# Value products of an attention stage in groups of four, three and three key tiles instead of two at a time

## The chip, the cores and the metric

The kernel runs on one core of one Trainium2 chip. The metric is the device time of the core in microseconds (us): the median over several executions. The kernel before takes 1477.8 us (median of 3 runs, 1475.59 to 1479.57).

## The reference

Two layers of a network over 1024 latent tokens behind a prefix of 256 context tokens, width 1024. Layer 0 mixes with gated recurrences and Fourier transforms; the change does not touch it. Layer 1 is attention with 16 heads, whose queries and keys have a part of 64 and a rotary part of 32, and whose output is gated and projected:

```python
def attend(q, k, v):
    s = jnp.einsum('bqhd,bkhd->bhqk', q, k, preferred_element_type=jnp.float32) * ATTN_SCALE
    p = jax.nn.softmax(s, axis=-1).astype(v.dtype)
    return jnp.einsum('bhqk,bkhd->bqhd', p, v)
...
    o_l = blocked_attention(q_l, k_all, v_all).reshape(b_, s_, MLA_WIDTH)
    y_lat = (o_l * jax.nn.silu(g_l)) @ w_out
```

The 1024 latent queries look at all 1280 keys; behind the attention come a residual and a layer normalisation.

## The kernel before

The attention stage works on 8 pairs of heads one after another (loop over `p`, L1116 on). A pair has two halves of 512 queries (`hf`), and a half has 10 key tiles of 128 keys (`kt`). The slot number `g` is 10 hf + kt, 0 to 19 within a pair. In the stage the order of work on TensorE, VectorE, ScalarE and GpSimd is the order in which the program issues it; each engine takes its own part in that order. The DMAs on the sync engine's queue (SP) are ordered by the framework.

At each key tile `attend` issues ten score matmuls into `s` (L1051): five products, each for the two heads of the pair in the upper and lower 64 rows of the array. ScalarE turns them into probabilities `p` (L1053, six buffers), and GpSimd adds these up into the row sums `ra` (L1057; in pair 7 GpSimd and VectorE share that, L1061, `ra` and `rv`). `pv` (L1067) issues the value products of one key tile: two matmuls, one for each head, each in its own 64 columns of the array, added up in `po`. A value matmul leaves two records in the trace. `finish` returns the rest of a half's work, which is issued in the next half at the key tiles named in its table: `rest` (the last value products and the product with the gate `sgt`, L1077), `rows` (the product of the row sums with ones, `rp`, L1084, copied to `ri` by ScalarE, L1087), four `piece` (a reciprocal of 128 columns each, L1092) and `last` (the product of `ri` and `sgt`, L1096, and the store to `o_dr`).

Between them stands work for the next pair, in the lists `near` (issued behind the scores) and `far` (issued last in a slot). The first slots have the key and query products (`pk`, `pq`), others the products of the next four heads (`pra`, `pv`, and on VectorE the scaling of `wk`, L882). From slot 2 on come the 24 units of `max_pass`: a unit multiplies 128 queries with 512 keys (or 256, every third) for the two heads (`mx`, L976) and VectorE reduces each head's tile to its maximum (`m`, L978). Behind the 24th, in slot 18, `mt` (L985) transposes the maxima `nm`. All these products take their tiles from one pool in turn:

```python
    m_ps, m_psc = pool("m_ps", 3, space=PSUM)
```

So a tile waits until the third tile before it has been read. `at_` is the table of the units' slots; an entry is the slot and 0 for `near`, 1 for `far`. One key tile is issued like this, with the value products of two key tiles at 3, 5, 7 and 9:

```python
                attend(p, hf, kt, st)
                for u in near[g]:
                    u()
                if kt > 2 and kt % 2:
                    pv(p, st, kt - 3)
                    pv(p, st, kt - 2)
                for u in tail.get(kt, ()):
                    u()
                for u in far[g]:
                    u()
```

Behind pair 7 stands the output projection `yf` (`out1`, L1191). Its first tile of tokens has the rest of the last half (`tail`) between its matmuls.

Of the kernel before, what the change touches and what calls it, by code (L numbers as in the profile page):

```python
# [27 lines left out]
NT = T // P  # L28
# [26 lines left out]
def _body(ctx, tc, ap, out, dbg=None):  # L55
# [947 lines left out]
    for m in range(8):  # L1003
# [3 lines left out]
        for q in range(2):  # L1007
            ps = s_ps.tile([P, 2, 512], F32, tag="s", name=f"in1g{m}{q}")[:, 0, :]
            c = slice(512 * q, 512 * q + 512)
# [54 lines left out]
    def pv(p, st, k):  # L1064
        q, i = divmod(p, 2)
        for a in range(2):
            TE.matmul(st["o"][64 * a : 64 * a + 64, :], quad[q][6][:, k, 128 * i + 64 * a : 128 * i + 64 * a + 64],  # L1067
                      st["e"][k][:, a, :], start=(k == 0), stop=(k == NT - 1), tile_position=(0, 64 * a))

    def finish(p, hf, st):  # L1070

        c = slice(512 * hf, 512 * hf + 512)

        def rest():
            for k in (8, 9):
                pv(p, st, k)
            V.tensor_tensor(out=st["sg"], in0=st["sg"], in1=st["o"], op=ALU.mult)  # L1077

        def rows():
            rp = m_ps.tile([P, 512], F32, tag="m", name=f"rp{p}{hf}")  # L1080
            sums = [st[n] for n in ("ra", "rv") if n in st]
            for j, r in enumerate(sums):
                for a in range(2):
                    TE.matmul(rp[64 * a : 64 * a + 64, :], ones, r[:, a, :], start=(j == 0), stop=(j == len(sums) - 1),  # L1084
                              tile_position=(0, 64 * a))
            st["ri"] = at.tile([P, 512], F32, tag="ri", name=f"ri{p}{hf}")
            S.copy(out=st["ri"], in_=rp)  # L1087

        def piece(b):
            def run():  # L1090
                d = slice(P * b, P * b + P)
                V.reciprocal(out=st["ri"][:, d], in_=st["ri"][:, d])  # L1092
            return run

        def last():
            V.tensor_tensor(out=st["sg"], in0=st["ri"], in1=st["sg"], op=ALU.mult)  # L1096
            load(o_dr[p][:, c], st["sg"])

        if p == 7 and hf == 0:
            return {1: [rest], 2: [rows], 3: [piece(0), piece(1)], 4: [piece(2)], 5: [piece(3), last]}  # L1100
        return {1: [rest], 3: [rows], 4: [piece(0)], 5: [piece(1)], 6: [piece(2)], 7: [piece(3)], 8: [last]}

    def o_load(t, p):
        orw = f1_p.tile([P, 8, P], F32, tag="raw", bufs=3, name=f"orw{t}")
# [4 lines left out]
        return oh, ol  # L1109

    vt[1] = at.tile([P, NT, 256], F32, name="v_odd")
    tail = {}
    for p in range(8):

# [2 lines left out]
        if p < 7:  # L1117
# [4 lines left out]
            near[1] += prep[3:4]  # L1122
            far[1] += prep[4:5]
            near[2] += prep[5:]
            at_ = [(g, b) for g in range(2, 2 * NT) for b in range(2) if not (g == 2 and b == 0) and (b == 0 or g % 2)]
            at_.insert(0, (2, 1))
            for (g, b), u in zip(at_, mx[:-1]):
                (far if b else near)[g].append(u)
            g = at_[len(mx) - 2][0]
# [34 lines left out]
        for hf in range(2):  # L1164
            st = {}
            for kt in range(NT):
                g = NT * hf + kt
                attend(p, hf, kt, st)
                for u in near[g]:
                    u()  # L1170
                if kt > 2 and kt % 2:
                    pv(p, st, kt - 3)
                    pv(p, st, kt - 2)
                for u in tail.get(kt, ()):
                    u()
                for u in far[g]:
                    u()
                if p == 7 and g == 18:
                    o0 = o_load(0, f1_p)
            tail = finish(p, hf, st)  # L1180
# [12 lines left out]

    H2 = [slice(0, 512), slice(512, D)]
    y0 = f_ps.tile([P, D], F32, tag="y", name="yf0")
    out1(*o0, [y0[:, c] for c in H2], H2, range(2), {1: tail[1], 3: tail[3]})
    for kt in sorted(tail)[2:]:
        for u in tail[kt]:
            u()
# [172 lines left out]
```

## Time and profile before

| What | Value |
|---|---|
| Median of 3 runs | 1477.8 us |
| The profiled execution | 1479.07 us |
| Its span, first to last instruction | 1477.3 us |
| Mean granted TensorE clock | 0.988 of full speed |
| Busy: TensorE, VectorE, ScalarE, GpSimd | 1409.1, 931.4, 539.9, 660.9 us |
| Attention stage, pairs 0 to 7 | about 842 to 1357 us |

All numbers are of one profiled execution. In a row of the timeline stand the start, the time from there to the end of the last of the merged instructions, the engine, the line, the operation with output and inputs, the shapes, how many instructions were merged, and in brackets how long the engine had been idle and what ended that. Matmuls overlap, so the distance of two starts tells what one costs. `DVE` is VectorE, `PE` TensorE, `ACT` ScalarE, `POOL` GpSimd.

### The profile page before, as it was taken

How to read it: one execution, taken by the hardware profiler on the slowest of the kernel's cores; microseconds unless marked ns; L12 is line 12 of the kernel's file. 1: busy time of each engine (PE TensorE's matmuls, PEld its weight loads, DVE VectorE, ACT ScalarE, POOL GpSimd, SP SyncE). 2: the span in 40 equal slices, each digit the busy share in tenths (PEclk: the TensorE clock that was granted, in tenths of full speed). 3: DMA queues.
4: the chain of work that ended last, by engine and by line, in shares of the span. 5: the costliest groups of instructions: out<-in, count | busy, mean ns of one | idle time of the engine just before them, and what ended most of it. 6: DMA issues, size and time to landing. Idle time of an engine off the chain costs nothing.

```text
span 1477.3 us, 19801 instructions
## 1 busy us (share of the span) xinstructions
PE 1409.1 (95%) x7912; PEld 1009.3 (68%) x7912; DVE 931.4 (63%) x1461; ACT 539.9 (37%) x664; POOL 660.9 (45%) x307
## 2 busy tenths in 40 slices
PE   6998999999999999998999999999999999998895
PEld 3776777787888788887976755655555555554674
DVE  5668878665765352239635365667566665767698
ACT  2276566666112221105421333443433434353110
POOL 1134334343211143303241187568767856675442
PEclk9999999999999999999999999999999999999998
DMA  8613233332303564210242211012101101033431
GB/s 307 232 51 110 97 111 111 111 103 76 123 29 126 188 192 140 92 52 22 89 137 71 72 33 51 15 37 59 39 22 38 57 16 37 15 95 113 159 131 74
DMA packets 65868, 134.09 MB, mean 91 GB/s; under 512 B 5864, under 2 KB 31720, under 8 KB 63472
## 3 DMA queue, kind: packets, MB, share of 16 engines
q1 hardware_dynamic: 63328, 124.83, 26.1%
q0 software_dynamic: 2016, 7.60, 1.4%
q8 instruction: 62, 1.02, 0.3%
q10 hardware_dynamic: 432, 0.39, 0.1%
q14 instruction: 30, 0.25, 0.1%
HBM read 101.14 MB, written 24.66 MB: 85 GB/s over the span
## 4 chain that ended last, share of the span: by engine, by line
PE 68%; DVE 20%; DMA 4%; issue 4%; ACT 2%; POOL 2%; SPq 0%; DVEq 0%; POOLq 0%; ACTq 0%
PE s L1051 11%; PE z L267 11%; PE y L646 10%; PE po L1067 9%; PE mx L976 6%; PE in1g L85 2%; PE in1g L87 2%; PE in1g L86 2%; DVE xc L317 2%; DVE hf L1246 1%; DVE th L362 1%; DVE gate L367 1%; DVE gate L378 1%; DVE hf L1236 1%; DMA woraw<-in_wo 1%
## 5 line engine op out<-in xcount | busy, mean ns | idle before, releaser
L1057 POOL TENSOR_TENSOR ra<-ra,p 128x1024 f32<-128x1024 f32 x112 | 269.2, 2403 | 96.3 <-ACT p L1053 93.1
L978 DVE TENSOR_REDUCE m<-mx 128x1 f32<-128x512 f32 (+1 forms) x384 | 210.1, 589 | 100.9 <-PE mx L976 100.5
L1053 ACT ACTIVATE p<-s 128x1024 f32<-128x1024 f32 x160 | 163.3, 1025 | 208.4 <-PE s L1051 208.3
L267 PE MATMUL z<-uh,w0h 128*128 128x512 f32 (+1 forms) x576 | 150.1, 368 | 4.3 <-ACT uh L76 4.3
L267 PE MATMUL z<-ul,w0h 128*128 128x512 f32 (+1 forms) x576 | 147.9, 362 | 0.0
L267 PE MATMUL z<-uh,w0l 128*128 128x512 f32 (+1 forms) x576 | 147.5, 361 | 0.0
L82 POOL TENSOR_TENSOR w0l<-w,w0h 128x1024 fp32r<-128x1024 f32 x24 | 63.9, 2664 | 185.4 <-DVE w0h L78 135.5
L267 PEld LDWEIGHTS z<-uh,w0h 128*128 128x128 f32 x576 | 98.7, 191 | 33.4 <-issue 10.7
L267 PEld LDWEIGHTS z<-ul,w0h 128*128 128x128 f32 x576 | 96.8, 190 | 18.6 <-issue 1.0
L267 PEld LDWEIGHTS z<-uh,w0l 128*128 128x128 f32 x576 | 96.4, 190 | 18.3 <-issue 2.0
L1051 PE MATMUL s<-R,KR 33*128 33x512 f32 (+1 forms) x640 | 101.5, 392 | 0.0
L345 ACT ACTIVATE gate<-gps,vec 128x512 f32<-128x512 f32 (+1 forms) x96 | 57.5, 616 | 104.3 <-PE gps L87 104.2
L976 PE MATMUL mx<-Kh,Qh 64*128 64x512 f32 (+1 forms) x384 | 83.4, 404 | 4.5 <-DVE m L978 4.5
L976 PEld LDWEIGHTS mx<-Kh,Qh 64*128 64x128 f32 x384 | 39.1, 185 | 69.4 <-DVE m L978 35.5
L1067 PE MATMUL po<-p,v_odd 128*64 128x512 f32 x320 | 77.5, 605 | 0.0
L1067 PE MATMUL po<-p,v_even 128*64 128x512 f32 x320 | 77.5, 605 | 0.0
L381 POOL TENSOR_TENSOR gate<-gate,gate 128x1280 f32<-128x1280 f32 x8 | 23.9, 2988 | 112.2 <-DVE gate L378 97.1
L976 PE MATMUL mx<-KR,R 64*128 64x512 f32 (+1 forms) x384 | 72.7, 356 | 0.0
L1051 PEld LDWEIGHTS s<-R,KR 33*128 33x128 f32 (+1 forms) x640 | 61.3, 184 | 13.1
L1051 PE MATMUL s<-Qh,Kh 64*128 64x512 f32 x320 | 69.9, 430 | 0.0
L649 DVE TENSOR_TENSOR n<-gbc,y 128x1024 f32<-128x1024 f32 x10 | 12.2, 1222 | 86.1 <-PE y L646 86.1
L1051 PE MATMUL s<-Ql,Kh 64*128 64x512 f32 x320 | 63.7, 391 | 0.0
(360 smaller groups left out, 3078.0 us busy)
## 6 DMA issues: line engine op xcount, KB each, us to landing
w<-in_w SPq DMA_DIRECT2D x24, 512.0 KB
adaw<-in_ada SPq DMA_DIRECT2D x32, 256.0 KB
adawm<-in_ada SPq DMA_DIRECT2D x8, 1024.0 KB
adawg<-in_ada_g SPq DMA_DIRECT2D x8, 1024.0 KB
y_dr<-sg SPq DMA_DIRECT2D x10, 640.0 KB
woraw<-in_wo SPq DMA_DIRECT2D x12, 512.0 KB
xt<-in_x_cm SPq DMA_DIRECT2D x8, 640.0 KB
yra<-y_dr SPq DMA_DIRECT2D x10, 512.0 KB
```

Of the source, the lines that this page charges most:

```text
L82: el.tensor_tensor(out=lo, in0=src, in1=f(hi), op=ALU.subtract)
L85: TE.matmul(o, lh, rh, start=start, stop=False)
L86: TE.matmul(o, lh, rl, start=False, stop=False)
L267: TE.matmul(z[:, a : a + n], wi[:, kt, :], ui[kt][:, a : a + n], start=(kt == 0 and ui is uh and wi is wh), stop=(kt == KT - 1 and wi is wl))
L345: S.activation(out=gt[d, g][:, a : a + n], in_=ps[:, :n], func=AF.Sigmoid, bias=vv("gateb", 4 * j + i))
L646: TE.matmul(ps[:, 512 * hf : 512 * hf + 512], a[k], b[k][:, 512 * hf : 512 * hf + 512], start=(k == 0 and a is yh and b is woh), stop=(k = ...
L976: TE.matmul(ps[a][:, :n], q[r, P * t : P * t + P], k[r, a0 : a0 + n], start=st, stop=not st)
L978: V.tensor_reduce(out=m3s[t][:, a, i : i + 1], in_=ps[a][:, :n], axis=AX.X, op=ALU.max)
L1051: TE.matmul(ps[:, a, :], k[r, ks], w[r, c], start=(j == 0), stop=(j == len(parts) - 1))
L1053: S.activation(out=es, in_=ps, func=AF.Exp, scale=SCALE)
L1057: G.tensor_tensor(out=ra, in0=st["e"][0] if kt == 1 else ra, in1=es, op=ALU.add)
L1067: TE.matmul(st["o"][64 * a : 64 * a + 64, :], quad[q][6][:, k, 128 * i + 64 * a : 128 * i + 64 * a + 64], st["e"][k][:, a, :], start=(k == ...
```

## The change

Value products are issued in three groups instead of five: those of key tiles 0 to 3 at key tile 5, those of 4 to 6 at key tile 8, and those of 7 to 9 in the next half at key tile 1. The product of the row sums moves from key tile 3 to 5, the four reciprocals from 4, 5, 6, 7 to 6, 7, 8, 9, and the last product from 8 to 9. In the table of the max units one `far` entry moves from slot 9 to slot 8. Between the two halves of pair 7 the table of `finish` stays as it is, but for the longer `rest`.

```diff
--- before.py
+++ after.py
@@ -1072,7 +1072,7 @@
         c = slice(512 * hf, 512 * hf + 512)
 
         def rest():
-            for k in (8, 9):
+            for k in PVL:
                 pv(p, st, k)
             V.tensor_tensor(out=st["sg"], in0=st["sg"], in1=st["o"], op=ALU.mult)
 
@@ -1098,7 +1098,7 @@
 
         if p == 7 and hf == 0:
             return {1: [rest], 2: [rows], 3: [piece(0), piece(1)], 4: [piece(2)], 5: [piece(3), last]}
-        return {1: [rest], 3: [rows], 4: [piece(0)], 5: [piece(1)], 6: [piece(2)], 7: [piece(3)], 8: [last]}
+        return {1: [rest], 5: [rows], 6: [piece(0)], 7: [piece(1)], 8: [piece(2)], 9: [piece(3), last]}
 
     def o_load(t, p):
         orw = f1_p.tile([P, 8, P], F32, tag="raw", bufs=3, name=f"orw{t}")
@@ -1109,6 +1109,9 @@
         return oh, ol
 
     vt[1] = at.tile([P, NT, 256], F32, name="v_odd")
+
+    PVG = {5: (0, 1, 2, 3), 8: (4, 5, 6)}
+    PVL = (7, 8, 9)
     tail = {}
     for p in range(8):
 
@@ -1122,8 +1125,7 @@
             near[1] += prep[3:4]
             far[1] += prep[4:5]
             near[2] += prep[5:]
-            at_ = [(g, b) for g in range(2, 2 * NT) for b in range(2) if not (g == 2 and b == 0) and (b == 0 or g % 2)]
-            at_.insert(0, (2, 1))
+            at_ = sorted([(g, 0) for g in range(3, 18)] + [(g, 1) for g in (2, 3, 5, 7, 8, 11, 13, 15, 17)])
             for (g, b), u in zip(at_, mx[:-1]):
                 (far if b else near)[g].append(u)
             g = at_[len(mx) - 2][0]
@@ -1168,9 +1170,8 @@
                 attend(p, hf, kt, st)
                 for u in near[g]:
                     u()
-                if kt > 2 and kt % 2:
-                    pv(p, st, kt - 3)
-                    pv(p, st, kt - 2)
+                for k in PVG.get(kt, ()):
+                    pv(p, st, k)
                 for u in tail.get(kt, ()):
                     u()
                 for u in far[g]:
@@ -1193,7 +1194,7 @@
 
     H2 = [slice(0, 512), slice(512, D)]
     y0 = f_ps.tile([P, D], F32, tag="y", name="yf0")
-    out1(*o0, [y0[:, c] for c in H2], H2, range(2), {1: tail[1], 3: tail[3]})
+    out1(*o0, [y0[:, c] for c in H2], H2, range(2), {1: tail[1], 3: tail[5]})
     for kt in sorted(tail)[2:]:
         for u in tail[kt]:
             u()
```

The places are shown in pair 1, second half. In the names `mx2710` is the max unit for pair 2, query tile 7, key piece 1, head 0; `s118` are the scores of pair 1, half 1, key tile 8; `p114` its probabilities of key tile 4. First TensorE at slot 17 (key tile 7), before:

```order
L976 MATMUL mx2710_7900<-Kh0_5775,Qh0_5773 128x512
L976 MATMUL mx2711_7901<-Kh0_5775,Qh0_5773 128x512
L976 MATMUL mx2710_7900<-KR1_5764,R10_5777 128x512
L976 MATMUL mx2711_7901<-KR1_5764,R10_5777 128x512
L1067 MATMUL po11_7663<-p114_7813,v_even_5769 64x512 x2
L1067 MATMUL po11_7663<-p115_7837,v_even_5769 64x512 x2
L976 MATMUL mx2720_7913<-Kh0_5775,Qh0_5773 128x256
L976 MATMUL mx2721_7914<-Kh0_5775,Qh0_5773 128x256
L976 MATMUL mx2720_7913<-KR1_5764,R10_5777 128x256
L976 MATMUL mx2721_7914<-KR1_5764,R10_5777 128x256
L1051 MATMUL s118_7922<-Qh1_6662,Kh1_6664 128x512 x2
```

and with the change:

```order
L976 MATMUL mx2710_7898<-Kh0_5775,Qh0_5773 128x512
L976 MATMUL mx2711_7899<-Kh0_5775,Qh0_5773 128x512
L976 MATMUL mx2710_7898<-KR1_5764,R10_5777 128x512
L976 MATMUL mx2711_7899<-KR1_5764,R10_5777 128x512
L976 MATMUL mx2720_7907<-Kh0_5775,Qh0_5773 128x256
L976 MATMUL mx2721_7908<-Kh0_5775,Qh0_5773 128x256
L976 MATMUL mx2720_7907<-KR1_5764,R10_5777 128x256
L976 MATMUL mx2721_7908<-KR1_5764,R10_5777 128x256
L1051 MATMUL s118_7916<-Qh1_6662,Kh1_6664 128x512 x2
```

The value group between the two units is gone: a unit of 512 keys is followed at once by one of 256, and that by the scores.

TensorE from slot 18 on, before:

```order
L985 MATMUL mt2_7936<-ident_60,nm2_7315 16x128
L1051 MATMUL s119_7944<-Qh1_6662,Kh1_6664 128x512 x2
L1051 MATMUL s119_7944<-Ql1_6663,Kh1_6664 128x512 x2
L1051 MATMUL s119_7944<-Qh1_6662,Kl1_6665 128x512 x2
L1051 MATMUL s119_7944<-R11_6666,KR1_5764 128x512 x2
L1051 MATMUL s119_7944<-R21_6667,KR2_5765 128x512 x2
L1067 MATMUL po11_7663<-p116_7873,v_even_5769 64x512 x2
L1067 MATMUL po11_7663<-p117_7897,v_even_5769 64x512 x2
```

and with the change:

```order
L985 MATMUL mt2_7930<-ident_60,nm2_7313 16x128
L1067 MATMUL po11_7661<-p114_7804,v_even_5769 64x512 x2
L1067 MATMUL po11_7661<-p115_7827,v_even_5769 64x512 x2
L1067 MATMUL po11_7661<-p116_7871,v_even_5769 64x512 x2
L1051 MATMUL s119_7943<-Qh1_6662,Kh1_6664 128x512 x2
```

The three value products of key tiles 4 to 6 now stand behind `mt`, and the group behind the scores of key tile 9 is gone.

VectorE over slots 16 to 18, before:

```order
L978 TENSOR_REDUCE m327_7876<-mx2700_7877 128x1
L978 TENSOR_REDUCE m327_7876<-mx2701_7878 128x1
L1092 RECIPROCAL ri10_7791<-ri10_7791 128x128
L978 TENSOR_REDUCE m327_7876<-mx2710_7900 128x1
L978 TENSOR_REDUCE m327_7876<-mx2711_7901 128x1
L1092 RECIPROCAL ri10_7791<-ri10_7791 128x128
L978 TENSOR_REDUCE m327_7876<-mx2720_7913 128x1
L978 TENSOR_REDUCE m327_7876<-mx2721_7914 128x1
L980 TENSOR_REDUCE nm2_7315<-m327_7876 128x2
L987 TENSOR_SCALAR mrow2_7938<-mt2_7936 16x128
L1096 TENSOR_TENSOR sgt10_7316<-ri10_7791,sgt10_7316 128x512
```

and with the change:

```order
L978 TENSOR_REDUCE m327_7874<-mx2700_7875 128x1
L978 TENSOR_REDUCE m327_7874<-mx2701_7876 128x1
L1092 RECIPROCAL ri10_7849<-ri10_7849 128x128
L978 TENSOR_REDUCE m327_7874<-mx2710_7898 128x1
L978 TENSOR_REDUCE m327_7874<-mx2711_7899 128x1
L1092 RECIPROCAL ri10_7849<-ri10_7849 128x128
L978 TENSOR_REDUCE m327_7874<-mx2720_7907 128x1
L978 TENSOR_REDUCE m327_7874<-mx2721_7908 128x1
L980 TENSOR_REDUCE nm2_7313<-m327_7874 128x2
L987 TENSOR_SCALAR mrow2_7932<-mt2_7930 16x128
L1092 RECIPROCAL ri10_7849<-ri10_7849 128x128 x2
L1096 TENSOR_TENSOR sgt10_7314<-ri10_7849,sgt10_7314 128x512
```

The reciprocals stand at the same two places among the reductions, but they are the first two pieces now (before, the last two), and two more follow ahead of the last product.

## Rows read from the trace of the kernel before

**Rows 1.** The page: busy time, share of span and instructions; the chain that ended last.

```profile
PE 1409.1 (95%) x7912; PEld 1009.3 (68%) x7912; DVE 931.4 (63%) x1461; ACT 539.9 (37%) x664; POOL 660.9 (45%) x307
...
PE 68%; DVE 20%; DMA 4%; issue 4%; ACT 2%; POOL 2%; SPq 0%; DVEq 0%; POOLq 0%; ACTq 0%
```

**Rows 2.** Windows view, pair 3: stretch, length, each engine's busy us, clock, DMA.

```profile
1040.40:1107.60 67.20, 67.20 (x438) 38.41 (x436) 41.73 (x74) 27.11 (x32) 45.53 (x20) 1.00 0.10 29
```

**Rows 3.** Timeline of TensorE, pair 6, slot 13 to the scores of slot 14.

```profile
1284.05 0.40 PE L1051 MATMUL s<-Qh,Kh 64*128 64x512 f32 x2
...
1285.21 0.40 PE L976 MATMUL mx<-Kh,Qh 64*128 64x512 f32 x2
1285.44 0.40 PE L976 MATMUL mx<-KR,R 64*128 64x512 f32 x2
1285.77 1.94 PE L1067 MATMUL po<-p,v_odd 128*64 128x512 f32 x8
1287.54 1.03 PE L1084 MATMUL rp<-ra,ones 128*64 128x512 f32 x4
1288.50 0.39 PE L976 MATMUL mx<-Kh,Qh 64*128 64x256 f32 x2
1288.72 0.28 PE L976 MATMUL mx<-KR,R 64*128 64x256 f32 x2
1288.84 0.39 PE L1051 MATMUL s<-Qh,Kh 64*128 64x512 f32 x2
```

**Rows 4.** Timeline of VectorE, the reductions of the unit at 1285.21.

```profile
1285.88 1.29 DVE L978 TENSOR_REDUCE m<-mx 128x1 f32<-128x512 f32 x2 [0.34 <-PE mx L976]
```

**Rows 5.** Timeline of TensorE, then VectorE, pair 2, slot 7.

```profile
998.65 0.39 PE L976 MATMUL mx<-Kh,Qh 64*128 64x512 f32 x1
1000.36 0.49 PE L976 MATMUL mx<-Kh,Qh 64*128 64x512 f32 x1 [1.32 <-DVE m L978]
...
1001.01 1.94 PE L1067 MATMUL po<-p,v_odd 128*64 128x512 f32 x8
...
996.98 2.72 DVE L882 TENSOR_SCALAR wk<-wk,vec 128x512 f32<-128x512 f32 x1
999.62 1.27 DVE L978 TENSOR_REDUCE m<-mx 128x1 f32<-128x512 f32 x2
```

**Rows 6.** Timeline of TensorE, pair 6, slot 9 to the scores of slot 10.

```profile
1275.59 0.38 PE L976 MATMUL mx<-Kh,Qh 64*128 64x256 f32 x1
1276.55 0.38 PE L976 MATMUL mx<-Kh,Qh 64*128 64x256 f32 x1 [0.58 <-DVE m L978]
...
1276.78 0.50 PE L1051 MATMUL s<-Qh,Kh 64*128 64x512 f32 x2
```

**Rows 7.** View of waits, 862 to 1350 us: total us, times, longest us.

```profile
PE mx L976 <- DVE m L978: 4.5, 4, 1.3
```

**Rows 8.** Timeline of VectorE, then TensorE, pair 6, slots 16 to 18.

```profile
1297.42 0.94 DVE L1092 RECIPROCAL ri<-ri 128x128 f32<-128x128 f32 x1
1298.28 1.22 DVE L978 TENSOR_REDUCE m<-mx 128x1 f32<-128x512 f32 x2
...
1300.28 0.69 DVE L978 TENSOR_REDUCE m<-mx 128x1 f32<-128x256 f32 x2
...
1301.21 0.28 PE L985 MATMUL mt<-ident,nm 128*16 128x128 f32 x1
```

**Rows 9.** View of line L1096: ns min, median, max; first and last start.

```profile
L1096 DVE TENSOR_TENSOR sgt<-ri,sgt x16: 669/1151/2781, 903.1 to 1371.0; 128x512 f32<-128x512 f32 x16
```

**Rows 10.** Timeline of VectorE, then TensorE, pair 3, slot 3.

```profile
1053.09 2.56 DVE L978 TENSOR_REDUCE m<-mx 128x1 f32<-128x512 f32 x4
...
1054.48 1.94 PE L1067 MATMUL po<-p,v_odd 128*64 128x512 f32 x8
```

**Rows 11.** Timeline of VectorE, then TensorE, pair 7 and its end.

```profile
1318.76 2.06 DVE L1061 TENSOR_TENSOR rv<-rv,p 128x1024 f32<-128x1024 f32 x1 [2.74 <-ACT p L1053]
...
1357.24 1.22 PE L1191 MATMUL yf<-w1oh,oh 128*128 128x512 f32 x2 [5.29 <-ACT oh L76]
```

## The prediction

> **What bounds the kernel now.** First the page: TensorE is busy 95% of the span, and the chain that ended last runs through it for 68% [rows 1]. Only the attention stage is touched, from about 842 us to 1375 us, so I read that stage pair by pair: in the 67.2 us of pair 3 TensorE is busy all the time, VectorE for 41.7 us, GpSimd for 45.5 us [rows 2]. An order of TensorE's work that has more gaps costs time one for one here, and one with fewer gains it; the other engines matter only where TensorE waits for them. The view of waits shows how little that is now: 4 waits of `mx` matmuls for VectorE, 4.5 us in all [rows 7]. Pair 7 is different: TensorE sits idle for 5.29 us before the output projection, and VectorE starts its `rv` work after 2.74 us of idleness and then stays busy [rows 11]; so VectorE, not TensorE, sets the end there.
>
> Durations below are of the profiled execution, 1479.07 us (its span of 1477.3 and 1.8 around it), 1.3 us over the median of the runs, 1477.8. I add the differences to the median.
>
> **The gain: fewer changes of tile shape.** Value products use two column tiles (128x64), scores and max products two row tiles (64x128). Entering a value group takes 0.33 us from the last `mx` start to the first `po` start, where the step within a shape is 0.23: 0.10 lost. Leaving costs twice: four records of `rp` take 0.96 where a record takes 1.77/8 = 0.22, so 0.08 lost, and the first 256-wide step afterwards is 0.22 instead of 0.12, 0.10 lost [rows 3]. Together 0.28 us a group. The order has 80 such groups before and 48 after: 28 fewer in pairs 0 to 6, on the path, 28 x 0.28 = 7.8 us, and 4 fewer in pair 7, which I cost at nothing, because VectorE sets the end there. The row sums' product stands directly behind a value group today already [rows 3], so that part saves nothing.
>
> **The loss: max units back to back.** Each pair runs 24 max units for the next one; eight slots hold two. Today a value group stands between the two at every one of them. Now the groups stand at key tiles 5 and 8 (and 1), and at key tiles 3 and 7 of both halves a 512-wide unit is followed at once by a 256-wide one. A unit takes two of the three buffers of `m_ps`, so the second unit's second tile needs the first unit's first buffer, and VectorE must have reduced that. The reduction starts 0.67 us after the unit's first matmul (1285.88 against 1285.21) and takes half of 1.29 us [rows 3, 4]; the waiting matmul starts 0.10 later (999.62 + 0.64 = 1000.26, against 1000.36) [rows 5]. So it starts at 0.67 + 0.64 + 0.10 = 1.41 us, and the scores follow 0.23 later (1276.55, 1276.78) [rows 6], at 1.64. Without a wait they would follow after two steps of 0.23 and two of 0.12, at 0.70. **Price: 0.94 us a place.** That TensorE really stops there is seen at 1000.36, where the same kind of tile waits while VectorE scales `wk` [rows 5]. At key tile 3 of the first half VectorE is already at work on four reductions: the third ends at 1053.09 + 3 x 0.64 = 1055.01, so the scores follow at 1055.34; with neither group nor wait they would at 1054.48 - 0.10 + 0.24 = 1054.62. There the price is 0.72 [rows 10]. With 4 places in each of 7 pairs that is 21 x 0.94 + 7 x 0.72 = 24.8 us. No row shows the pairing itself; the nearest are this 0.72 and the 1.8 us lost around 1000.36 (998.65 to 1001.01 is 2.36, where 0.46 + 0.10 would do). Between them I take the composed 0.94, since its three parts are measured.
>
> The Trainium skill has a rule against this change: TensorEngine Tiling (Array Packing), section PSUM Bottleneck, says that tiling speeds TensorE up but not the emptying of PSUM, which may then be the limit. The wait at 1000.36 agrees; by the rule the loss counts whole, and without it the sum would be the gain alone.
>
> **VectorE is later where the groups are gone.** The four reciprocal pieces (0.86 us from start to next start) move from key tiles 4 to 7 to key tiles 6 to 9, so that pieces fall where no value group covers them.
> - *Slots 16 to 18.* From the start of the unit at 16: its reductions run from 0.67 to 1.96, a piece to 2.82 [rows 4, 8]. The unit at 17 starts at 0.46 + 1.16 = 1.62 [rows 3], its first half is reduced at 3.46, and the scores follow at 3.79 instead of 2.32. VectorE ends the second half at 4.10, another piece at 4.96, the 256-wide pair (0.69) at 5.65, and `mt`, which stood 0.24 behind that pair, comes at 5.89; TensorE would be there at 3.79 + 1.16 + 0.10 = 5.05 [rows 3, 8]. Lost 1.47 + 0.84 = 2.31, of which 0.94 is counted: 1.37 x 7 = 9.6 us.
> - *Slots 6 to 8.* In odd pairs `pv` products after unit 6 give VectorE time for the first piece; after unit 7 the second runs to 2.82, the next reduction ends at 3.17, and unit 8 waits till 3.27 instead of 2.80: 0.47 x 3. Pair 6 has no such products: 0.50 + 0.47. Pairs 2 and 4 scale `wk` at this place, 2.72 us [rows 5], and lose the 1.8 there today; depending on whether the scaling takes half of that or all, the same walk gives -0.1 to +0.9 more, taken 0.4 each. Pair 0 has no pieces in its first half: -0.9. Sum 2.3 us.
> - *Slots 9 to 11.* The last product of a half (L1096) takes 0.67 to 2.78 us, median 1.15 [rows 9], and now comes right before units 10 and 11. At the short end nothing waits, at the long end 1.4 us is lost; I take 0.5 x 6, less the 0.85 that one of them costs today (1276.78 - 1275.59, less 0.34) [rows 6]: 2.1 us.
>
> L1096 has two inputs in SBUF. The Trainium skill, GPSIMD Engine Reference, Key points, says that GpSimd and VectorE instructions of that kind contend for SBUF; the spread in its row agrees, and by the rule the long end would hold wherever an addition to the row sums runs.
>
> **Pair 7.** The third key tile of the last group (4 x 0.22 = 0.9 us) moves behind the first projection matmuls and ahead of the last row sums, on which the end hangs: +0.9. Scores reach key tile 5 with 8 records and one group less before them, 2.0 us earlier; VectorE's 2.74 us of idleness can use it. I take 1.2, as ScalarE has weight casts between its exponentials, against 0.9 for the piece that moves behind: -0.3. Sum +0.6.
>
> **Costed at nothing.** The probabilities have six buffers: tile 0 is released at key tile 5, one ahead of the exponential that takes its buffer, and tiles 4 to 6 at key tile 8, two ahead. GpSimd's additions get two key tiles more before the row sums need them. On SP the store of a half moves one key tile later and the rotary copies queue behind it, by about 1 us; they are read first by the max unit in slot 2. If that cover fell short, 1 us a pair would be lost.
>
> **Sum:** -7.8 + 24.8 + 9.6 + 2.3 + 2.1 + 0.6 = **+31.6 us**; 1477.8 + 31.6 = 1509.
>
> **Rivals.**
> 1. *Only the gain counts* (the other side). The second unit finds its buffers free, because the reductions keep pace. 1477.8 - 7.8 + 0.6 = 1471. It decides at 7.8/28 = 0.28 us a place: below that the change wins. For it: VectorE is idle for a third of a pair [rows 2], and there are few waits today [rows 7]. Against: the 1.41 us to the release is arithmetic on three rows, and the wait at 1000.36 is of this very kind. Chance 0.10. The Trainium skill's TensorEngine Tiling (Array Packing), Key Properties, says that a change of tiling mode drains TensorE; that agrees with the 0.28, and taken alone it leads here.
> 2. *They cancel.* The places cost a third of what I say: 1478. Chance 0.06.
> 3. *Short waits.* 0.72 at every place, 20.2 us, the pieces fit into VectorE's idle time, and the 1.8 lost in pairs 0, 2 and 4 today goes into the new waits: -7.8 + 20.2 - 5.4 + 0.6 = +7.6, 1485; without the last, 1491. Chance 0.10.
> 4. *VectorE becomes the bound.* L1096 at its long end six times (8.4 in place of 3.0) and the scaling at its full length (+1.5): 1516; if also 14 of the places, those with pieces, cost 1.8: +12, 1528. Chance 0.14.
> 5. *The change does not do what it says.* The order shows the groups and the adjacent units as described, so I leave nothing for it.
>
> **How the numbers follow.** The forecast has 0.60; its own range is 1493 to 1516. With rival 3 and most of rival 4 it becomes 1484 to 1526 for 8 in 10. About 0.3%, 4.4 us, is what a measurement of this kernel can tell from no change. Faster by more: 0.10 (rival 1). Within: 0.06 (rival 2). Slower: 0.84.
>
> **What would show it.** Right: a pair of about 71.5 us in place of 67.2; some 28 `mx` waits for VectorE in place of 4, each right behind another `mx` unit; `mt` late after unit 17; value groups of 16 and 12 records with the same 0.28 at their edges. Wrong: pairs under 67 us with adjacent units at 0.7 us (rival 1), or TensorE waiting for exponentials instead.

## The result and the profile after

The changed kernel takes 1518.97 us (median of 4 runs, 1518.59 to 1521.57), the kernel before 1478.68 beside it (4 runs): a ratio of 1.0274, 95% interval 1.0254 to 1.0294. It is slower, by 40 us where 31.6 were forecast. The profiled execution took 1519.03 us, 39.96 more than that of before. The result lies in the wide range of the forecast (1484 to 1526) and above its own (1493 to 1516).

The page of the kernel after: busy time, the chain of waits, and the group of the max products (busy us, mean ns | idle before them, what ended most of it).

```profile
PE 1425.8 (94%) x7912; PEld 1027.9 (68%) x7912; DVE 929.6 (61%) x1461; ACT 540.8 (36%) x664; POOL 659.0 (43%) x307
...
PE 68%; DVE 23%; issue 3%; DMA 2%; ACT 2%; POOL 1%; SPq 0%; DVEq 0%; POOLq 0%; ACTq 0%
...
L976 PE MATMUL mx<-Kh,Qh 64*128 64x512 f32 (+1 forms) x384 | 98.9, 403 | 26.8 <-DVE m L978 26.5
```

The engines do the work they did [rows 1]. VectorE's share of the chain has grown from 20% to 23%, 1.8 us less of busy time notwithstanding. TensorE's 16.7 us more of busy time are no more work either: it is the same 7912 matmuls. The group of `mx` has 26.8 us of idleness ahead of its products, 26.5 of it for VectorE's maxima; before, the same row has 4.5.

The view of waits of after, 862 to 1350 us (us, times, longest), answers to [rows 7]:

```profile
PE mx L976 <- DVE m L978: 26.2, 33, 1.6
PE mt L985 <- DVE nm L980: 4.2, 7, 0.6
```

Instead of 4 waits of `mx` there are 33 in this stretch, and a 34th ahead of it: one at each of the 28 adjacent places, and six in slot 11, where no unit follows another directly. `mt` waits in each of the seven pairs. The timeline of TensorE and VectorE, pair 6, slots 17 and 18, shows one of them; it answers to [rows 8]:

```profile
1332.33 0.39 PE L976 MATMUL mx<-Kh,Qh 64*128 64x512 f32 x2
...
1332.57 0.94 DVE L1092 RECIPROCAL ri<-ri 128x128 f32<-128x128 f32 x1
1332.79 0.30 PE L976 MATMUL mx<-Kh,Qh 64*128 64x256 f32 x1
1333.43 1.22 DVE L978 TENSOR_REDUCE m<-mx 128x1 f32<-128x512 f32 x2
1334.11 0.38 PE L976 MATMUL mx<-Kh,Qh 64*128 64x256 f32 x1 [1.02 <-DVE m L978]
...
1336.36 0.38 PE L985 MATMUL mt<-ident,nm 128*16 128x128 f32 x1 [0.61 <-DVE nm L980]
1336.68 4.33 PE L1067 MATMUL po<-p,v_odd 128*64 128x512 f32 x12
```

The second unit issues one product at 1332.79, 0.46 behind the first unit, and stands still until VectorE has reduced the first unit's first tile. VectorE comes to that only behind a reciprocal. At 1336.36 `mt` waits for the last maxima. The group of 12 value records behind it takes 4.33 us, where the same group in pair 3 takes 2.79: here the granted clock is 0.50 (1336.5 to 1339.5 us).

Windows view of after, pair 3 (length, busy us of TensorE, its weight loads, VectorE, ScalarE, GpSimd, clock, DMA), beside the 67.20 us of [rows 2]:

```profile
1052.60:1125.11 72.51, 68.45 (x439) 40.74 (x437) 41.97 (x74) 27.13 (x32) 42.79 (x18) 1.00 0.09 27
```

The pair is 5.3 us longer at the same full clock. TensorE stands still for 72.51 - 68.45 = 4.06 of it; the rest is counted as busy, although the work is the same, with two value groups fewer in each half.

**Where the 39 us lie.** I took the start of each slot's first score matmul in both traces and subtracted slot lengths. From the first pair to the first `yf` the difference is 39.06 us. By pair, 0 to 7, it is +1.08, +5.31, +6.33, +5.34, +6.30, +5.16, +8.62 and +0.92. The value products that only changed places are taken out at the prediction's own prices (0.22 a record, 0.28 a group); what is left over pairs 0 to 6, in us, is:

| Slots | What stands there | Forecast | Measured |
|---|---|---|---|
| 0 to 5 | adjacent units at 3 | 5.0 | 5.8 |
| 6 to 9 | adjacent units at 7, pieces, `wk` | 8.0 | 3.9 |
| 10 to 12 | `last` ahead of units 10 and 11 | 3.0 | 15.8 |
| 13 to 15 | adjacent units at 13 | 6.6 | 6.4 |
| 16 to 19 | adjacent units at 17, pieces, `mt` | 16.2 | 15.1 |

The five forecasts hold the 0.94 and 0.72 of the adjacent places and the terms for the pieces; the 0.85 that pair 6 gets back is in the second. The measured column sums to 46.9 before rounding; less 8.7 for the 28 groups and the records that move over into pair 7, and with the 0.92 of pair 7, that is the 39.06 again. One row stands out: slots 10 to 12.

**Slots 10 to 12.** Timeline of after, pair 2, GpSimd, VectorE and TensorE:

```profile
1017.96 2.38 POOL L1057 TENSOR_TENSOR ra<-ra,p 128x1024 f32<-128x1024 f32 x1 [3.87 <-ACT p L1053]
...
1018.79 2.10 DVE L1096 TENSOR_TENSOR sgt<-ri,sgt 128x512 f32<-128x512 f32 x1
...
1019.54 0.39 PE L976 MATMUL mx<-Kh,Qh 64*128 64x512 f32 x1
...
1020.81 2.57 DVE L978 TENSOR_REDUCE m<-mx 128x1 f32<-128x512 f32 x4
1021.54 0.49 PE L976 MATMUL mx<-Kh,Qh 64*128 64x512 f32 x1 [1.62 <-DVE m L978]
...
1022.20 4.49 PE L1067 MATMUL po<-p,v_odd 128*64 128x512 f32 x12
```

An addition of the row sums runs on GpSimd from 1017.96 to 1020.34. The last product of the half (L1096) starts within it, and ends at 1020.89, 0.55 behind its end: 2.10 us instead of the 0.67 of its short end. This is regular: in the two traces 26 of its executions begin while a GpSimd instruction runs and take longer than 0.7 us, and each ends 0.55 behind the end of that instruction; one that GpSimd starts after it does not hold it. So its time is what is left of the running instruction, and 0.55. The reductions that TensorE needs queue behind it, and unit 11 waits 1.62. The same happens in all six pairs that have this product before units (2.08 to 2.10 us each), and the view of the line (ns min, median, max), beside [rows 9], has a median of 1790 in place of 1151:

```profile
L1096 DVE TENSOR_TENSOR sgt<-ri,sgt x16: 693/1790/2097, 904.6 to 1411.6; 128x512 f32<-128x512 f32 x16
```

In odd pairs the products of the next values stand between, so 1.5 us are lost; in pairs 2, 4 and 6 it is 2.1, and then a second thing follows. Windows view of the same place in pair 2 (the column behind the busy times is the granted clock):

```profile
1019.00:1022.00 3.00, 1.38 (x12) 0.71 (x8) 3.00 (x3) 0.20 (x1) 3.00 (x2) 1.00 0.00 0
1022.00:1024.00 2.00, 2.00 (x9) 0.60 (x8) 1.38 (x3) 0.61 (x2) 1.28 (x2) 0.59 0.34 85
1024.00:1026.00 2.00, 2.00 (x8) 0.57 (x6) 0.00 (x0) 0.93 (x2) 1.92 (x2) 0.55 0.78 282
1026.00:1028.00 2.00, 2.00 (x18) 1.24 (x16) 1.26 (x3) 0.00 (x0) 1.69 (x1) 1.00 0.47 158
```

TensorE was busy for 1.38 of 3.00 us, and behind that the granted clock is 0.59 and 0.55 for 4 us, near the lower level, 1.2 of 2.4 GHz. The twelve value records take 4.49 us, 1.70 more than the usual 2.79. In pairs 0 to 6 there are four such falls, at slot 11 of pairs 2, 4 and 6 and at slot 18 of pair 6, about 6.6 us in all; before, there is none.

**Slots 6 to 9.** Here less was lost than forecast. Timeline of after, VectorE and GpSimd, pair 2:

```profile
1004.37 0.48 DVE L882 TENSOR_SCALAR wk<-wk,vec 128x512 f32<-128x512 f32 x1
...
1005.58 1.29 POOL L82 TENSOR_TENSOR wkl<-wk,wkh 128x512 fp32r<-128x512 f32 x1 [1.73 <-ACT wkh L76]
```

The scaling of `wk`, 2.72 us before [rows 5], takes 0.48, because GpSimd is idle for the 1.73 us before 1005.58: the additions have been shifted by the change. In pair 0 it takes 0.64. The stop of 1.8 us that pairs 0, 2 and 4 had at this place is gone. The odd pairs, which have no scaling, lose 1.3 us each in slots 6 to 9, as forecast (0.94 + 0.47).

### The profile page after: what moved, and what is told of

Its sections match the earlier page's. It is cut to its first block, busy times and chain, and to the rows that moved or that the text cites. A ratio compares the mean times of both kernels' runs of the same rounds, so it can differ in the third digit from the quotient of the medians.

```text
span 1517.3 us, 19797 instructions
## 1 busy us (share of the span) xinstructions
PE 1425.8 (94%) x7912; PEld 1027.9 (68%) x7912; DVE 929.6 (61%) x1461; ACT 540.8 (36%) x664; POOL 659.0 (43%) x307
## 3 DMA queue, kind: packets, MB, share of 16 engines
q8 instruction: 62, 1.02, 0.3%
## 4 chain that ended last, share of the span: by engine, by line
PE 68%; DVE 23%; issue 3%; DMA 2%; ACT 2%; POOL 1%; SPq 0%; DVEq 0%; POOLq 0%; ACTq 0%
PE z L267 13%; PE po L1067 10%; PE s L1051 10%; PE y L646 10%; PE mx L976 5%; DVE m L978 4%; PE in1g L85 2%; PE in1g L87 2%; PE in1g L86 2%; DVE xc L317 2%; DVE ri L1092 2%; DVE hf L1247 1%; DVE th L362 1%; DVE gate L367 1%; DVE gate L378 1%
## 5 line engine op out<-in xcount | busy, mean ns | idle before, releaser
L976 PE MATMUL mx<-Kh,Qh 64*128 64x512 f32 (+1 forms) x384 | 98.9, 403 | 26.8 <-DVE m L978 26.5
L976 PEld LDWEIGHTS mx<-Kh,Qh 64*128 64x128 f32 x384 | 47.3, 185 | 86.1 <-DVE m L978 50.3
L1051 PE MATMUL s<-R,KR 33*128 33x512 f32 (+1 forms) x640 | 104.6, 392 | 0.0
L976 PE MATMUL mx<-KR,R 64*128 64x512 f32 (+1 forms) x384 | 83.8, 367 | 0.0
L1051 PE MATMUL s<-Qh,Kh 64*128 64x512 f32 x320 | 73.1, 429 | 0.5 <-ACT p L1053 0.4
L1051 PEld LDWEIGHTS s<-R,KR 33*128 33x128 f32 (+1 forms) x640 | 65.6, 184 | 10.7
L1051 PE MATMUL s<-Ql,Kh 64*128 64x512 f32 x320 | 67.0, 391 | 0.0
L1051 PE MATMUL s<-Qh,Kl 64*128 64x512 f32 x320 | 66.8, 390 | 0.0
```

Of the source, the lines that this page charges most:

```text
L976: TE.matmul(ps[a][:, :n], q[r, P * t : P * t + P], k[r, a0 : a0 + n], start=st, stop=not st)
L1051: TE.matmul(ps[:, a, :], k[r, ks], w[r, c], start=(j == 0), stop=(j == len(parts) - 1))
```

## The experiments

The theory: adjacent units cost 0.94 (0.72) a place, late pieces and `last` cost the rest, and grouping as such gains. The rivals: adjacency is harmless and something else costs; grouping gains nothing; VectorE's time beside GpSimd is what decides.

**1. Only the adjacency, in the kernel before** (`e1_adjacent_only`). The value groups stay as they were; the second unit of four slots is issued ahead of the group.

```diff
+                if p < 7 and g in (3, 7, 13, 17):
+                    far[g].pop(0)()
                 if kt > 2 and kt % 2:
```

> The kernel before, with one edit: in slots 3, 7, 13 and 17 of pairs 0 to 6 the second max unit is issued ahead of the value group instead of behind it. Groups, reciprocals and the table of finish stay as before. Theory (back-to-back max units wait for VectorE to free a buffer of m_ps): some 0.94 us at 21 places and 0.72 at 7, 24 us together, so about 1502 us against 1478, and 28 more waits of mx for VectorE. Rival (the larger value groups are the cause, and units that touch cost nothing): 1478, within 4 us.

Measured: 1516.68 us, ratio 1.0249 (1.0227 to 1.0270): 36 us, 12 more than the theory's 24.8. Slot 3 is longer by 0.72, slots 7 and 13 of odd pairs by 0.95, slot 17 by 1.31, and each slot behind by 0.1. At 0.72 and 0.95 the two composed prices are met; in slot 13 of pairs 0, 2 and 4 it is only 0.52. Slot 17 costs more, since a reciprocal stands ahead of the reductions there; and pairs 0, 2 and 4 lose 1.2 to 2.5 more at slot 7, where `wk` is scaled and the clock falls behind the stop. The view of waits, 862 to 1350:

```profile
PE mx L976 <- DVE m L978: 23.5, 31, 1.3
```

So adjacency alone, with no group removed and no piece moved, makes a loss at the price worked out, and more where it meets the scaling of `wk`; the first rival of the prediction falls.

**2 and 3. The units taken away from both kernels.** The 256-wide second units of slots 3, 7, 13 and 17 are left out (so 256 of the 1280 keys are missing from the maxima of four of eight query tiles): no unit follows another there, with the change or without it.

```diff
             def run():
+                if i == 2 and p and t in (0, 2, 5, 7):
+                    return
...
```

> The changed kernel, leaving out the four 256-wide max units of each pair 1 to 7 that stand in slots 3, 7, 13 and 17 behind another unit (the maxima of those query tiles are then taken over 1024 of the 1280 keys). It is to be read against the kernel before with the same units left out. Theory: without units that touch, what is left of the change is the gain of 7.8 us from fewer changes of shape, against the waits of slots 9 to 12 (11 us) with the falls of the granted clock behind them (6.6 us where they come): 0 to +10 us over its counterpart, about 1472 to 1482. Rival (larger groups are the cause): 35 us or more over its counterpart.

> The kernel before, leaving out the same four 256-wide max units of each pair 1 to 7 as its counterpart. Both theories: 28 x 0.24 us of matmuls less, and some of the waits in slot 7, so 1478 - 7 to - 11, about 1467 to 1472.

Measured: 1494.72 us (1.0099, 1.0076 to 1.0122) with the change and 1471.51 (0.9947, 0.9928 to 0.9967) without: 23 us apart, with no adjacent unit left. The kernel before met its 1467 to 1472. The changed one fits neither side: I expected it 0 to 10 us over its twin, the rival 35 or more. In odd pairs the difference is only 0.89 a pair; the rest is in even ones. Timeline of the changed kernel, pair 2, slot 5, GpSimd, VectorE and TensorE:

```profile
990.99 4.82 POOL L1061 TENSOR_TENSOR ra<-ra,p 128x1024 f32<-128x1024 f32 x2 [1.02 <-ACT p L1057]
...
991.83 4.19 DVE L879 TENSOR_SCALAR wq<-wq,vec 128x384 f32<-128x384 f32 x2
...
993.01 0.39 PE L978 MATMUL mx<-Kh,Qh 64*128 64x512 f32 x1
995.94 1.27 DVE L980 TENSOR_REDUCE m<-mx 128x1 f32<-128x512 f32 x2
996.68 0.79 PE L978 MATMUL mx<-Kh,Qh 64*128 64x512 f32 x1 [3.27 <-DVE m L980]
```

With the units gone everything comes at another moment. Now, in pairs 0, 2 and 4, it is the scaling of `wq` (0.74 for the two when GpSimd was idle in the kernel before) that falls into two GpSimd additions and takes 4.19, and a max unit behind it waits 3.27. Slot 11 lost as much as in the change itself (+2.45 odd, +4.6 even). A removed cause had let another one in.

**4. The change with the old finish table** (`e4_change_tail_early`): row sums, pieces and `last` where they were; the value groups as in the change.

```diff
-        return {1: [rest], 5: [rows], 6: [piece(0)], 7: [piece(1)], 8: [piece(2)], 9: [piece(3), last]}
+        return {1: [rest], 3: [rows], 4: [piece(0)], 5: [piece(1)], 6: [piece(2)], 7: [piece(3)], 8: [last]}
```

> The changed kernel with the table of finish from the kernel before: the row sums' product back at key tile 3, the reciprocals at 4 to 7, the last product at 8. The row sums' product then stands between the two max units of slots 3 and 13, and the last product has the value group of slot 8 behind it. Theory: the waits of slots 3 and 13 go (10 us), those of slot 11 and the falls of the clock go (17 us), 14 more changes of shape come (4 us): about 1496 us against 1519. Rival (larger groups are the cause): 1519, within 4 us.

Measured: 1498.77 us (1.0124, 1.0099 to 1.0149), 20 us under the change (22 by the ratios), where 23 were expected. Slot by slot against the change, slots 11 are shorter by 16.1 us together. Against the kernel before they are longer by 0.87 now, which is the moved value records and nothing else: the wait is gone. Slots 3 and 13 give back another 4.2, since the product of the row sums now stands between their two units. So this run does not take adjacency and the late work quite apart; experiment 5 does. Slots 16 to 19 cost what they cost in the change, but for falls of the clock, although the reciprocals are back at their old key tiles: two of them stand at slots 16 and 17 in either table. What was worth moving back was `last`, not the reciprocals. The 14 waits of `mx` that are left in the view are those of slots 7 and 17:

```profile
PE mx L976 <- DVE m L978: 12.8, 14, 1.0
PE mt L985 <- DVE nm L980: 4.1, 7, 0.6
```

**5. `last` on GpSimd** (`e5_change_last_on_gpsimd`): the change, with the product of L1096 on the engine that it collides with.

```diff
-            V.tensor_tensor(out=st["sg"], in0=st["ri"], in1=st["sg"], op=ALU.mult)
+            (G if p < 7 else V).tensor_tensor(out=st["sg"], in0=st["ri"], in1=st["sg"], op=ALU.mult)
```

> The changed kernel with one edit: the last product of a half (ri times sgt) runs on GpSimd instead of VectorE in pairs 0 to 6. Theory: in slots 9 to 11 VectorE's product, with two inputs in SBUF, takes 2.1 us because an addition of GpSimd runs; the max units of slot 11 wait for it (1.5 us in odd pairs, 2.1 in pairs 2, 4, 6), and behind the longer waits the granted clock falls (1.7 us each). On GpSimd it stands in nobody's way: 11 us of waits and 5 us of clock go, about 1503 us against 1519. Rival (the three value products in slot 11 are the cause, not VectorE): 1519, within 4 us.

Measured: 1506.45 us (1.0178, 1.0155 to 1.0201), 12.5 under the change (14 by the ratios). Timeline, pair 2, slot 11, VectorE, TensorE and GpSimd:

```profile
1018.25 1.22 DVE L978 TENSOR_REDUCE m<-mx 128x1 f32<-128x512 f32 x2
...
1019.10 0.39 PE L976 MATMUL mx<-Kh,Qh 64*128 64x512 f32 x2
...
1019.65 2.79 PE L1067 MATMUL po<-p,v_odd 128*64 128x512 f32 x12
...
1019.88 1.26 POOL L1096 TENSOR_TENSOR sgt<-ri,sgt 128x512 f32<-128x512 f32 x1
...
1025.37 0.50 PE L1051 MATMUL s<-Qh,Kh 64*128 64x512 f32 x2 [0.87 <-ACT p L1053]
```

The reductions follow at once, unit 11 does not wait, and twelve value records take 2.79. Against the change, slot 11 is shorter by 1.56 in odd pairs and by 3.81 in pairs 2, 4 and 6, which is the whole wait and the whole clock loss. That shows what slots 10 to 12 had cost: 3 x 1.56 + 3 x 3.81 = 16.1 us. The value products of slot 11 are still there, so the rival falls. The run shows that L1096 in VectorE's queue is the cause; that GpSimd's addition stretches it rests on the durations above. Part comes back at slot 12 of pairs 2 and 4 (1.03 each), where a score waits 0.87 for an exponential, and three falls of the clock now stand at slot 18, where the change had one. 1503 was expected.

**6 to 8. The scalings on GpSimd too.** Experiment 2, its twin, and the whole kernel before, each with `last` and the scalings of the next weights on GpSimd:

```diff
...
-            V.tensor_scalar(out=u, in0=u, scalar1=vv("kvng"), scalar2=None, op0=ALU.mult)
+            (G if q else V).tensor_scalar(out=u, in0=u, scalar1=vv("kvng"), scalar2=None, op0=ALU.mult)
...
```

> The changed kernel without the four second units of each pair (left out as in the earlier run) and with the last product and the scalings of the weights of pairs 2 to 7 on GpSimd, so that VectorE has no work left that waits for GpSimd next to the max units. To be read against its counterpart made of the kernel before. Theory: what is left is the gain from 32 fewer changes of shape, 0.28 us each, less 0.9 at the end: 7 us under its counterpart, some 1458 us. Rival (larger groups cost time by themselves): at or over its counterpart.

> The kernel before without the same four units and with the same products on GpSimd. Both theories: the 1.8 us of slot 7 in pairs 0, 2, 4 and the 0.85 in slot 9 of pair 6 go: about 1471.5 - 6 = 1465 us.

> The kernel before, whole, with the last product and the scalings of the weights of pairs 2 to 7 on GpSimd. Theory: the waits of max units that the kernel before has, 1.8 us in slot 7 of pairs 0, 2 and 4 and 0.85 in slot 9 of pair 6, go: 6 us under the kernel before, 1473 against 1479. Rival (GpSimd, with more to do, holds the probabilities longer): no gain, or slower.

Measured: 1481.70 us (1.0011, 0.9996 to 1.0026), 1469.24 (0.9933, 0.9915 to 0.9951) and 1477.64 (0.9983, 0.9970 to 0.9997). Against experiment 2 the move gains 13 us, but the changed one is still 12.5 over its twin, not 7 under it. View of waits, 862 to 1350, of the sixth, and its GpSimd and ScalarE in pair 2, slot 7:

```profile
PE s L1055 <- ACT p L1057: 13.5, 6, 4.3
PE mt L989 <- DVE nm L982: 5.4, 7, 0.8
...
998.86 1.57 POOL L882 TENSOR_SCALAR wk<-wk,vec 128x512 f32<-128x512 f32 x1
1000.46 0.62 ACT L76 CAST wkh<-wk 128x512 fp32r<-128x512 f32 x1 [4.97 <-POOL wk L882]
```

No `mx` product waits any more. Six scores wait instead, five of them in pairs 0, 2 and 4, up to 4.3 us for exponentials: ScalarE's cast of `wk` waits for GpSimd's scaling, which queues behind additions, and the next exponential stands behind the cast. In odd pairs, which have no scaling, the changed kernel gains 0.73 a pair, although `mt` waits 0.77 in each: by that estimate grouping gains about 1.5 a pair. The seventh was expected at 1465 and stays 4 over it. The eighth, the whole kernel before, was to gain 6 us and gains 3: its slot 7 is shorter by 0.6 in pairs 2 and 4, not by the full 1.8, for the same reason, and slot 12 is longer by 0.8 there. What it gains lies in slot 9 of pair 6 (0.85) and at the end of pair 7 (1.8).

**9 to 12. The casts issued later, and a milder grouping.** The cast and split of `wk` become a unit of their own, issued in slot 12. The twelfth run is the kernel before with this and the moves to GpSimd; the tenth and eleventh are the sixth and seventh with it:

```diff
-        return [w_scale, lambda: split(wh, wl, w, S, G), k_scale], ra(0) + ra(1)
+        return [w_scale, lambda: split(wh, wl, w, S, G), k_scale, lambda: split(kh, kl, u, S, G)], ra(0) + ra(1)
...
-                for g, u in zip((3, 4, 5, 8, 9, 10, 13, 14, 15), w3 + r6):
+                for g, u in zip((3, 5, 5, 12, 8, 9, 10, 13, 14, 15), w3 + r6):
```

The ninth run adds to the twelfth four value groups a half instead of five, keeping a group between all units except those of slot 9:

```diff
-            for k in (8, 9):
+            for k in (8, 9) if p == 7 and hf else (6, 7, 8, 9):
...
-                if kt > 2 and kt % 2:
+                if kt > 2 and kt % 2 and (kt < 9 or p == 7 and hf):
```

> The kernel before, whole, with the last product and the scalings on GpSimd and the casts issued later: the part of the candidate that is not the grouping. Theory: the waits of slot 7 in pairs 0, 2, 4 (5.4 us) go and nothing takes their place: 1473 to 1474 against 1479. Rival: as with the early cast, within 2 us of the kernel before.

> The kernel before, whole, with four value groups a half in place of five (key tiles 3, 5, 7, and the last four value products in the next half at key tile 1; the last half of pair 7 as it was), so that only the unit pair of slot 9 loses its cover, and that unit is moved to the end of slot 8, behind other products. The last product of a half and the scalings of the next weights run on GpSimd, and ScalarE's casts behind them are issued later. My theory (a group less gives 0.28 us; units back to back cost; VectorE work beside a GpSimd addition costs what is seen at wk): 14 groups x 0.28 = -4, the waits of slot 7 in pairs 0, 2, 4 gone (-5), the wait of slot 9 in pair 6 gone (-0.8), new short waits at slots 8 and 9 +2: about 1471 against 1479. Rival (groups give nothing, the waits only move): 1477 to 1480. If ScalarE's casts still hold exponentials up: over 1480.

> The change without the second units of slots 3, 7, 13, 17 (256 of the 1280 keys are left out of the maxima of four of the eight query tiles), with the last product and the scalings on GpSimd, and the cast of wk issued later than in the run of this kind before, where it held exponentials up in even pairs. Left in this pair of runs is the grouping alone. Theory: 28 groups x 0.28 = 7.8 less what mt and short waits take (odd pairs gave -0.73 each before, pair 6 -0.49): 5 to 7 us under its twin without the change. Rival (grouping gives nothing): no difference. If it is slower than its twin, the groups cost something that I have not named.

> The twin: the kernel before without the same second units and with the same moves to GpSimd and the late cast. Theory: about 1469, as the run of this kind with the early cast, or 1 to 2 us under it.

Measured, beside 1481.37 us for the kernel before (17 runs):

| Run | us | Ratio to before, 95% interval |
|---|---|---|
| `e12_before_gp_late` | 1471.95 | 0.9936, 0.9916 to 0.9956 |
| `e9_four_groups` | 1477.39 | 0.9973, 0.9958 to 0.9987 |
| `e10_change_less_units_late` | 1466.78 | 0.9898, 0.9876 to 0.9919 |
| `e11_before_less_units_late` | 1464.93 | 0.9892, 0.9871 to 0.9913 |

*The twelfth* is the best whole kernel: 9.4 us under the kernel before, more than the 5 to 6 expected. Its slot 7 is shorter by 1.8 in pairs 0, 2 and 4, slot 9 of pair 6 by 0.84, and no `mx` product waits in the attention stage. The end of pair 7 is shorter by 1.7, too, which was not forecast. Timeline, pair 2, slot 7, in place of the stop in [rows 5]:

```profile
997.12 1.94 PE L1066 MATMUL po<-p,v_odd 128*64 128x512 f32 x8
997.47 1.56 POOL L882 TENSOR_SCALAR wk<-wk,vec 128x512 f32<-128x512 f32 x1
997.67 1.22 DVE L977 TENSOR_REDUCE m<-mx 128x1 f32<-128x512 f32 x2
```

The scaling runs on GpSimd in 1.56 us and the reductions in their usual 1.22 beside it.

*The ninth* was to be at 1471 and is at the rival's number, 5.4 us over the twelfth: the milder grouping loses, too. Its gain is there: 8 value records take 1.97 us out of slot 19 and add 1.71 to slot 1, so the group that is gone was worth 0.26. But slot 0 of pairs 1 to 6 is longer by 0.75 to 0.84. Timeline of TensorE there, pair 1:

```profile
902.02 0.80 PE L1050 MATMUL s<-R,KR 64*128 64x512 f32 x3
903.03 0.49 PE L1050 MATMUL s<-R,KR 33*128 33x512 f32 x1 [0.21 <-DMA R<-mrow]
```

The first scores of a pair need the row of maxima, which `mt` and a DMA bring into `R`. Before, the value group of key tile 9 stood between `mt` and these scores; without it they come 1.97 us earlier and wait for the DMA. In the change itself three key tiles stand behind `mt`, and slot 0 loses nothing. Pair 7 is 4.84 longer; 1.77 of that are the value records that come over from pair 6. Another 1.75 lie between the last scores and the output projection. Timeline of VectorE and ScalarE there, the ninth run and then the twelfth:

```profile
1346.63 1.90 DVE L1095 TENSOR_TENSOR sgt<-ri,sgt 128x512 f32<-128x512 f32 x1
1354.79 1.04 ACT L76 CAST oh<-orw 128x1024 fp32r<-128x1024 f32 x1 [5.89 <-DMA orw<-o_dr]
...
1339.96 1.89 DVE L1095 TENSOR_TENSOR sgt<-ri,sgt 128x512 f32<-128x512 f32 x1
1348.20 1.04 ACT L76 CAST oh<-orw 128x1024 fp32r<-128x1024 f32 x1 [4.14 <-DMA orw<-o_dr]
```

The cast that the projection waits for comes 6.3 us behind the end of pair 7's `last` of the first half in both, and in the ninth run that product ends 1.8 us later, counted from the last scores. So 1.75 of the 5.4 us hang on when VectorE is through with this product, and not on TensorE's order. The remaining 1.3 us are not traced to a cause.

*The tenth and eleventh* isolate the grouping: 1.85 us apart by their medians, the changed one not ahead. So the expected 5 to 7 are not there, and the rival (no difference) has the sum right. By slots the price is there: in odd pairs the tenth gains only 0.07 a pair, but 0.79 is lost in slot 2 and 0.68 in slots 16 to 19. Without these it would gain 0.07 + 0.79 + 0.68 = 1.54, for four groups less: 0.38 a group. Waits and one row of TensorE's timeline, pair 1, slot 2:

```profile
PE mt L988 <- DVE nm L981: 3.2, 5, 0.8
PE mx L977 <- DMA R<-roth: 1.9, 3, 0.6
```

```profile
913.94 0.50 PE L977 MATMUL mx<-KR,R 64*128 64x512 f32 x1 [0.62 <-DMA R<-roth]
```

The rotary copy into `R` comes late in the three odd pairs, and `mt` waits again. Pair 7 is 1.54 longer, 0.88 of it for records that come over from pair 6. The 0.38 is an estimate, since both losses are taken out of it. With the adjacent units gone and the products that met GpSimd moved off VectorE, the change's 40 us shrink to 2; the gain of grouping is taken by the next thing that was just in time.

## Why the prediction was right, and where it was off

- *Sign and mechanism.* Right. TensorE bounds the stage, and the added time is TensorE waiting for VectorE, as in [rows 5] but 34 times. The change alone does not tell adjacency from the late tail; experiments 1 and 5 do.
- *The price of a place, 0.94 and 0.72.* Right: 0.95 and 0.72 in experiment 1, and 6.4 us against 6.6 in slots 13 to 15 of the change, where beside it only TensorE products change places. It is an average there: 0.8 in even pairs, 1.0 in odd ones. The Trainium skill's rule in TensorEngine Tiling (Array Packing), PSUM Bottleneck, that the emptying of PSUM may be the limit, agrees with these waits.
- *The gain, 0.28 a group.* Right: 0.26 in slots 19 and 1 of the ninth run, and by estimate 0.38 in odd pairs of the tenth and eleventh. My first rival, in which this gain alone counts, is excluded: even with every adjacent unit gone the sum did not show it.
- *Slots 16 to 18, +9.6.* Nearly right in size: slots 16 to 19 lose 1.92 a pair against 2.31, plus one fall of the clock of 1.64. The move of the reciprocals, which the prediction names, has no part in it: with them back (experiment 4) the loss is the same. Experiment 1, with every reciprocal and group in its place, has 1.31 of it from the adjacency at slot 17; the other 0.6 is the wait of `mt`, which has no value group ahead of it any more.
- *Slots 6 to 8, +2.3.* Too high: the place came to 3.9 against 8.0 us, nearly all of it in pairs 0, 2 and 4. I had the scaling of `wk` at half or all of its 2.72; it took 0.48, since the additions that stretched it had moved. Its cost was a matter of what GpSimd does at that moment, and I carried the old moment over.
- *Slots 9 to 11, +2.1.* **This is the step that failed.** I took 0.5 us a pair, between the short and the long end of L1096, for a product that now comes right ahead of units 10 and 11. It takes 2.08 to 2.10 every time there, and 1.5 to 2.1 are lost, with 1.7 for the clock in three pairs: 15.8 us instead of 3.0. The fourth rival had it at its long end six times, 8.4; the clock was in none of the cases.
- *Pair 7, +0.6.* Right: 0.92.
- *Costed at nothing.* The copies on SP and the buffers of the probabilities held in the change: slots 0 to 2 lose nothing. That this cover is thin the tenth run shows: there the rotary copy does come late, for 0.79 in each odd pair, where I had given 1.
- *What was to be seen.* A pair of 71.5 us came out as 72.5 (odd) and 73.5 (pairs 2 and 4), 28 `mx` waits as 34, of which six are not behind another unit, and `mt` is late in all seven.

The two large errors, 12.8 us too little at slots 10 to 12 and 4.1 too much at slots 6 to 9, have opposite signs, and the other terms together were 1.2 too much. That the sum came within 8.4 us of the profiled difference is in part luck; 0.9 of the 8.4 lies outside the stretch up to `yf`. The first half of rival 4, 1516, came nearest: its L1096 at the long end was as measured, its scaling at full length was not.

## What to carry to other kernels

Work that looks like a costly change of shape between two producers may be the cover under which their consumer frees buffers; before removing it, count producers against buffers and walk the consumer's time from release to release. An instruction whose row spreads from 0.67 to 2.78 us has two prices: look which neighbour ran at each end, and ask what runs at its new place; the median is the price of neither. Here the price could be worked out: what is left of GpSimd's running instruction, and 0.55 us. If an experiment that removes a cause shows a new loss, read which instruction moved into whose time before giving up the theory, and try the cure for that neighbour by itself: here it was worth more than the grouping.

## What the runs showed of the hardware that was not expected

- *VectorE beside GpSimd.* The scaling of `wk` takes 0.48 us with GpSimd idle and 2.72 with a subtraction on GpSimd still running for 0.1 us and an addition starting 0.03 behind it; the two of `wq` 0.74 and 4.19. L1096, with two inputs in SBUF, ended 0.55 us behind the addition at 1020.34, as in 25 more executions, as if it began its own work only when GpSimd was through. The prediction's rule (the Trainium skill, GPSIMD Engine Reference, Key points) is borne out, and a second one is sharper: SBUF — State Buffer, Who interferes with whom, says that some VectorE instructions with one input share a port pair with GpSimd as well, and that one side then waits for the whole instruction of the other. The scalings agree with that. The reductions, which read PSUM, keep their 1.22 to 1.29 beside additions.
- *TensorE's clock in a busy stretch.* Stops of 1.6 us in an otherwise full stretch were followed by some 4 us at 0.55 to 0.59 of the clock, 1.5 to 1.7 us of loss each. In the change this happened behind each of the three stops of 1.6 us, and once at slot 18 of pair 6, behind two shorter ones (1.02 and 0.61) that pairs 0 to 5 had as well, without a fall. Which stops are followed by one the runs do not settle.
